# A decoder layer on one core: tokens instead of weights on the stationary side of the two MLP products

## The chip, the core and the metric

The kernel runs on one core of a Trainium2 chip. The metric is the device time in microseconds of one execution, as the median of three runs. The profile is of one further execution, taken by the hardware profiler; its span, from the first to the last instruction, is a little shorter than the device time of the same execution.

## What is computed

One layer of a hybrid decoder for 256 tokens (and 16 learned meta tokens ahead of them) of width 2048, all in float32. The part that matters here is the MLP at the end:

```
h = h + hybrid_mixer(rmsnorm(h, norm_mix_g), ...)        # two attention branches, gates, output projection
h = h + squared_relu_mlp(rmsnorm(h, norm_mlp_g), w1, w2)
return rmsnorm(h, final_norm_g)[:, 16:]

def squared_relu_mlp(xn, w1, w2):                         # w1: 2048 x 8192, w2: 8192 x 2048
    return square(relu(xn @ w1)) @ w2
```

The meta tokens are dropped, so the MLP works on 256 tokens.

## The kernel before

**Number format.** Every float32 operand is cut into an upper part `hi` (float32r) and a rest `lo`, and a product is the sum of hi·hi, hi·lo and lo·hi. ScalarE (ACT) makes `hi` with a cast, VectorE (DVE) makes `lo` with a subtraction.

**Layout.** Features lie on the partitions, tokens along the free dimension. A block of 128 output features and all 2048 input features is one weight *chunk* of 1 MB, stored as sixteen 128x128 tiles, one for each k-step `k`. The stationary operand of each matmul is a weight tile, the moving operand is the activation row `x[:, k]` with 512 columns: 256 tokens of `hi` and 256 of `lo`. `mac2` (L148) issues two matmuls for a k-step:

```
nc.tensor.matmul(steps(ps), hi, steps(row(x)), ...)                 # L149: weight hi, 512 columns
nc.tensor.matmul(steps(ps[:, 0:NT]), lo, steps(x[:, 0, :]), ...)    # L150: weight lo, 256 columns
```

`steps` (L141) reads and writes the columns in an order of four passes. `gemm2` (L160) does the 16 k-steps of a chunk into one PSUM bank. The left half of the bank and the right half are added afterwards.

**Weights.** `next_weights` (L131) takes the next chunk of one long list in two halves. Each half is one 512 KB transfer on the SyncE (SP) queue into a `raw` tile (L124; five of them), one cast on ACT (L126, 128x1024) and one subtraction on DVE (L127, 128x1024) into a `w` tile (five of them too).

**Stages.** The input products, the attention branches and the output projection come first (to about 845 us). The MLP then goes over four groups `g` of 2048 hidden features. In each group 16 chunks of `w1` give 16 hidden features blocks (operand `x2`), and 16 chunks of `w2` give 16 blocks of the output (operand `a`). A hidden block goes through `relu2` (L891): `total` adds the two halves of the bank (ACT copy L187, DVE add L190), DVE takes the maximum with zero times `r2b`, the row of inverse norms (L893), squares it (L895), and `split_to` writes hi (ACT, L194) and lo (DVE, L195) into `a`. An output block is added to the residual `h` by `add_residual` (L870: ACT copy L872, DVE adds L873 and L874).

**The end.** In the last group each of the output blocks 0 to 11 is also squared into `acc` (ACT L867, GpSimd (POOL) L868) and multiplied by the final gain (ACT L915). For the last four chunks the `lo` products come first (L927), with `hi` kept in `whi_last`, and then `half` (L931) does the `hi` products for 128 tokens after the other 128 (L943), so that the final norm of the first 128 tokens (`row`, L961: L967 sums `acc` over the partitions on TensorE) and their output go beside the products of the second.

**Order.** Each engine runs its own list in order. The lists are made by a scheduler that may move an instruction ahead of others on the same engine. Weight transfers are the only work of the SP queue in the MLP, and POOL's queue has none there.

## Time and profile before

| | |
|---|---|
| median of 3 runs | 1534.97 us (1534.77 to 1535.41) |
| the profiled execution | 1535.16 us |
| its span | 1533.5 us |
| TensorE clock granted | 0.998 |
| busy share of the span | PE 99%, weight load 91%, DVE 70%, ACT 52%, POOL 8% |
| read from HBM | 289.32 MB, 190 GB/s over the span |

How to read it: PE is TensorE's matmuls, PEld its weight loads (LDWEIGHTS), which overlap the matmuls. A matmul's duration in the profile is longer than the distance to the next one's start, because matmuls are pipelined; what a matmul costs is read from starts. In a group's row the numbers behind `|` are busy time, mean ns of one, and idle time of the engine just before the group's instructions with what ended it. The chain of waits is the sequence of work that ended last, followed back from the end.

### The profile page before, as it was taken

Reading aid. Unit: us, or ns where it says so; the run is one execution under the profiler, and the core shown is the slowest. Engines: PE = TensorE matmul, PEld = TensorE weight load, DVE = VectorE, ACT = ScalarE, POOL = GpSimd, SP = SyncE. Lnnn points to the kernel's source line nnn. Section 1 sums busy time; section 2 is a strip of 40 time slices with the busy share of each in tenths; the row PEclk is TensorE's granted clock in tenths of the full one; section 3 lists DMA queues with packets and bytes.
Section 4 is the critical chain, followed back from the end, with each engine's and each line's share of the span. In section 5 each row is a group of like instructions: output and inputs, shape, how many; then the busy total and the mean of one; then the engine's idle time right before and its main releaser. Section 6 shows DMA issues by size and latency. Waiting matters only on the chain.

```text
span 1533.5 us, 25353 instructions
## 1 busy us (share of the span) xinstructions
PE 1522.3 (99%) x9812; PEld 1399.9 (91%) x9812; DVE 1072.2 (70%) x1659; ACT 794.4 (52%) x1271; POOL 130.2 (8%) x213
## 2 busy tenths in 40 slices
PE   9999999999999999999999999999999999999997
PEld 8999999999999999999999999999999999999997
DVE  7898858586666666666787876667766776667665
ACT  7766444555555544544666544445444454444563
POOL 6012010111100000000011000000000000000012
PEclk9999999999999999999999999999999999999999
DMA  9545555565555565655565566655565556555562
GB/s 320 172 153 176 182 162 188 160 212 170 166 167 188 197 198 197 195 199 199 188 209 195 197 198 197 200 195 195 195 203 197 198 196 199 197 197 200 194 195 96
DMA packets 86600, 293.08 MB, mean 191 GB/s; under 512 B 9112, under 2 KB 16800, under 8 KB 86352
## 3 DMA queue, kind: packets, MB, share of 16 engines
q1 hardware_dynamic: 85872, 289.62, 57.4%
q8 instruction: 77, 1.26, 0.3%
q0 software_dynamic: 176, 1.12, 0.2%
q10 hardware_dynamic: 432, 0.72, 0.1%
q14 instruction: 43, 0.35, 0.1%
HBM read 289.32 MB, written 2.11 MB: 190 GB/s over the span
## 4 chain that ended last, share of the span: by engine, by line
PE 96%; DVE 2%; ACT 1%; issue 1%; DMA 0%; POOL 0%; SPq 0%; POOLq 0%; DVEq 0%; ACTq 0%
PE ps L149 50%; PE ps L150 26%; PE psa L154 5%; PE psa L158 4%; PE psa L156 4%; PE ps L364 1%; PE ps L943 1%; PE ps L366 1%; DVE w L127 1%; PE ps L927 0%; DMA raw<-w_all_dram 0%; PE pa L562 0%; PE po L620 0%; DVE room L434 0%; POOL o L991 0%
## 5 line engine op out<-in xcount | busy, mean ns | idle before, releaser
L127 DVE TENSOR_TENSOR w<-raw,w 128x1024 fp32r<-128x1024 f32 x522 | 644.8, 1235 | 260.5 <-ACT w L126 251.3
L126 ACT CAST w<-raw 128x1024 fp32r<-128x1024 f32 x522 | 547.1, 1048 | 275.2 <-PE ps L150 210.1
L149 PE MATMUL ps<-x,w 128*128 128x512 f32 x1952 | 654.7, 381 | 0.0
L150 PE MATMUL ps<-x,w 128*128 128x256 f32 x1952 | 535.7, 274 | 0.0
L149 PEld LDWEIGHTS ps<-x,w 128*128 128x128 f32 x1952 | 366.5, 188 | 62.4
L150 PEld LDWEIGHTS ps<-x,w 128*128 128x128 f32 x1952 | 366.7, 188 | 0.0
L149 PE MATMUL ps<-a,w 128*128 128x512 f32 x960 | 320.2, 380 | 0.0
L150 PE MATMUL ps<-a,w 128*128 128x256 f32 x960 | 263.3, 274 | 0.0
L149 PEld LDWEIGHTS ps<-a,w 128*128 128x128 f32 x960 | 180.3, 188 | 30.9
L154 PE MATMUL psa<-x,w 128*128 128x272 f32 x640 | 181.9, 285 | 0.0
L150 PEld LDWEIGHTS ps<-a,w 128*128 128x128 f32 x960 | 180.3, 188 | 0.0
L158 PE MATMUL psa<-x,w 128*128 128x272 f32 x640 | 179.8, 282 | 0.0
L156 PE MATMUL psa<-x,w 128*128 128x272 f32 x624 | 176.1, 282 | 0.0
L187 ACT COPY evb<-ps 128x256 f32<-128x256 f32 x160 | 59.4, 371 | 205.1 <-PE ps L150 203.5
L190 DVE TENSOR_TENSOR evt<-ps,evb 128x256 f32<-128x256 f32 x158 | 67.0, 424 | 80.1 <-ACT evb L187 79.7
L154 PEld LDWEIGHTS psa<-x,w 128*128 128x128 f32 x640 | 120.2, 188 | 0.2
L158 PEld LDWEIGHTS psa<-x,w 128*128 128x128 f32 x640 | 120.2, 188 | 0.1
L156 PEld LDWEIGHTS psa<-x,w 128*128 128x128 f32 x624 | 117.6, 188 | 0.0
L868 POOL TENSOR_TENSOR acc<-acc,hsq 128x256 f32<-128x256 f32 x26 | 26.5, 1017 | 737.6 <-ACT hsq L867 737.6
L149 PE MATMUL ps<-og,w 128*128 128x512 f32 x256 | 85.8, 380 | 0.0
L149 PE MATMUL ps<-y,w 128*128 128x512 f32 x256 | 85.4, 380 | 0.0
L872 ACT COPY evb<-ps 128x256 f32<-128x256 f32 x76 | 28.2, 371 | 103.3 <-PE ps L150 102.3
(297 smaller groups left out, 1471.2 us busy)
## 6 DMA issues: line engine op xcount, KB each, us to landing
raw<-w_all_dram SPq DMA_DIRECT2D x537, 512.0 KB, 4.5
raw<-w_all_dram SPq DMA_DIRECT2D x8, 384.0 KB, 6.7
h<-hT_dram SPq DMA_DIRECT2D x8, 275.0 KB, 6.8
negc<-fdram POOLq DMA_DIRECT2D x1, 1088.0 KB, 7.9
out_dram<-o SPq DMA_DIRECT2D x2, 512.0 KB, 2.6
raw<-w_all_dram SPq DMA_DIRECT2D x2, 256.0 KB, 3.7
room<-w_small_dram SPq DMA_DIRECT2D x1, 320.0 KB, 8.1
out_dram<-o ACTq DMA_DIRECT2D x1, 320.0 KB, 3.1
```

The source lines that it names most:

```text
L126: nc.scalar.copy(hi[:, k, :], r)
L127: nc.vector.tensor_tensor(lo[:, k, :], r, hi[:, k, :].bitcast(F32), op=ALU.subtract)
L149: nc.tensor.matmul(steps(ps), hi, steps(row(x)), start=first, stop=False)
L150: nc.tensor.matmul(steps(ps[:, 0:NT]), lo, steps(x[:, 0, :]), start=False, stop=last)
L154: nc.tensor.matmul(steps(ps[:, X_LO]), hi, steps(x_lo[:, k]), start=first, stop=False, skip_group_check=True)
L156: nc.tensor.matmul(steps(ps[:, 0:NA]), lo, steps(x_hi[:, k]), start=False, stop=last and hi is None, skip_group_check=True)
L158: nc.tensor.matmul(steps(ps[:, 0:NA]), hi, steps(x_hi[:, k]), start=False, stop=last, skip_group_check=True)
L187: nc.scalar.copy(b, ps[:, NT:512])
L190: nc.vector.tensor_tensor(t, ps[:, 0:NT], b, op=ALU.add)
L364: nc.tensor.matmul(steps(ps), hi, steps(row(x[:, k])), start=st, stop=False)
L868: nc.gpsimd.tensor_tensor(acc, acc, sq, op=ALU.add)
L872: nc.scalar.copy(b, ps[:, NT:512])
```

## The change

For both MLP products the sides are exchanged. The stationary operand is now a tile of 128 tokens and 128 input features (`x[:, k, o, P*t : P*t+P]`, token half `t`, `o` hi or lo), and the moving operand is a row of 512 weight columns, four chunks wide. `token_rows` does a *block* of four chunks: for each k-step and token half three matmuls of 512 columns, hi·hi, hi·lo and lo·hi, into one PSUM bank for each token half. With `n=2` two blocks go together: k-steps 0 to 11 of the one, 0 to 11 of the other, then 12 to 15 of each.

`wide_weights` loads, casts and subtracts two k-steps of four chunks at a time; a tile has the same 1024 columns a partition as before, in pieces of 256 columns (1 KB) from four chunks.

The products now have tokens on the partitions, so they are turned. `turn` transposes 32x32 squares on DVE into a tile, writes that to DRAM in four transfers and reads it back in one; all five are on POOL's queue. For the hidden features `hidden` does it per block, after ACT has taken relu with the scale `r2` (now one number per token and partition) and the square. For the output, `gathered` sums the rows of each block over the groups in `rows`, and turns each block once, at the last group for blocks 0 and 1 and at the last but one for blocks 2 and 3; POOL then adds them to `h`. The last group's output blocks 2 and 3 (chunks 8 to 15) are done as before, the last four of them in the two halves as before.

`norm2` sums over the partitions with the ones as moving operand (two columns). Start offsets of `x2`, `a`, `whi_last` and some weight tiles move by 32 columns. 32 chunks x 4 groups of matmuls become 30 blocks of token rows (16 for `w1`, 14 for `w2`) and 8 chunks of the old form.

```diff
+    def wide_weights(c0, q):
+        k0 = 4 * q
+        parts = []
+        for i in range(2):
+            raw = wp.tile([P, HK * P], F32, tag="raw", name=nm("raw"), bufs=RAW)
+            hi, lo = (t.rearrange("p k m -> p (k m)").rearrange("p (k c m) -> p k c m", k=2, m=P) for t in pair())
+            r = raw.rearrange("p (c k m) -> p c k m", k=2, m=P)
+            cols = slice((k0 + 2 * i) * P, (k0 + 2 * i + 2) * P)
+            nc.sync.dma_start(r, w_all[c0 : c0 + 4, :, cols].rearrange("c p (k m) -> p c k m", m=P))
+            r = r.rearrange("p c k m -> p k c m")
+            nc.scalar.copy(hi, r)
+            nc.vector.tensor_tensor(lo, r, hi.bitcast(F32), op=ALU.subtract)
+            parts.append([t.rearrange("p k c m -> p k (c m)") for t in (hi, lo)])
+        return lambda k: tuple(t[:, k % 2, :] for t in parts[k % 4 // 2])
...
-    x2 = operand(keep, "x2", at=56, tag="s2")
+    x2 = operand(keep, "x2", at=24, tag="s2")
...
+    def token_rows(x, n, between=None):
+        pts = [[bank(px, "pt") for _ in range(2)] for _ in range(n)]
+        for i, q in [(i, q) for i in range(n) for q in range(3)] + [(i, 3) for i in range(n)]:
+            w = wide_weights(chunk[0] + 4 * i, q)
+            for k in range(4 * q, 4 * q + 4):
+                hi, lo = w(k)
+                for t, ps in enumerate(pts[i]):
+                    xh, xl = (x[:, k, o, P * t : P * t + P] for o in range(2))
+                    nc.tensor.matmul(steps(ps), xh, steps(hi), start=(k == 0), stop=False)
+                    nc.tensor.matmul(steps(ps), xh, steps(lo), start=False, stop=False)
+                    nc.tensor.matmul(steps(ps), xl, steps(hi), start=False, stop=(k == KT - 1))
...
+    def turn(rows):
+        both = gat.tile([P, KT * P], F32, tag="o", name=nm("turn"))
+        for t, r in enumerate(rows):
+            nc.vector.transpose(both[:, 0:1024].rearrange("p (i t j r) -> p t i j r", i=4, t=2, r=32)[:, t],
+                                r().rearrange("p (j i s) -> p i j s", i=4, s=32))
+        back = both[:, 1024:]
+        there = dram.tile([P, 1024], F32, tag="there", name=nm("there"), bufs=2)
+        for c in range(4):
+            nc.gpsimd.dma_start(there.rearrange("(i s) (c e) -> c s i e", i=4, c=4)[c],
+                                both[32 * c : 32 * c + 32, 0:1024].rearrange("s (i e) -> s i e", i=4))
+        nc.gpsimd.dma_start(back, there)
+        return back.rearrange("p (c t j r) -> p j t c r", c=4, t=2, r=32)
+
+    def hidden(a, b, pt):
+        u = gat.tile([P, 2, 512], F32, tag="u", name=nm("u"), bufs=1)
+        def part(t):
+            nc.scalar.activation(u[:, t, :], pt[t], AF.Relu, scale=r2[:, 2 * t : 2 * t + 1])
+            nc.scalar.activation(u[:, t, :], u[:, t, :], AF.Square)
+            return u[:, t, :]
+        back = turn([lambda t=t: part(t) for t in range(2)])
+        for t in range(2):
+            hi, lo = (a[:, 4 * b : 4 * b + 4, o, P * t : P * t + P].rearrange("p j (c r) -> p j c r", r=32) for o in range(2))
+            split_to(hi, lo, back[:, :, t])
+
+    def gathered(g, b, pt):
+        rs = [rows[:, t, 512 * b : 512 * b + 512] for t in range(2)]
+        for r, ps in zip(rs, pt):
+            if g == 0:
+                nc.scalar.copy(r, ps)
+            else:
+                nc.vector.tensor_tensor(r, ps, r, op=ALU.add)
+        if g < (NG - 1 if b < 2 else NG - 2):
+            return
+        back = turn([lambda r=r: r for r in rs])
+        for j in range(4 * b, 4 * b + 4):
+            r = ht[:, j, :].rearrange("p (t c r) -> p t c r", t=2, r=32)
+            nc.gpsimd.tensor_tensor(r, r, back[:, j - 4 * b], op=ALU.add)
+            if b < 2:
+                normed(j)          # square_sum(j, acc) and the final gain
...
     for g in range(NG):
-        a = operand(keep, "a", at=16, tag="s1")
-        held = []
-        for f in range(KT):
-            ps = gemm2(next_weights(), x2, pool=px if g == 0 and f < 3 else pg)
...
-            relu2(a, f, ps)
-        last = g == NG - 1
-        for j in range(KT - NL if last else KT):
-            add_residual(j, gemm2(next_weights(), a))
...
+        a = operand(keep, "a", at=48, tag="s1")
+        for b in range(4):
+            hidden(a, b, *token_rows(x2, 1, norm2 if (g, b) == (0, 0) else None))
+        for b0, n in ((0, 2),) if g == NG - 1 else ((0, 2), (2, 1), (3, 1)):
+            for b, pt in enumerate(token_rows(a, n), b0):
+                gathered(g, b, pt)
+    for j in range(8, KT - NL):
+        add_residual(j, gemm2(next_weights(low=True), a))
+        normed(j)
```

**What TensorE has to do, in the middle of a group.** Before, the last k-step of one hidden block and the first of the next (`ps` is the PSUM bank; 128x4x32x4 is 512 columns, 128x4x16x4 is 256):

```order
L149 MATMUL ps_1427_9902<-x2_1211_8413,w_1426_9898 128x4x32x4
L150 MATMUL ps_1427_9902<-x2_1211_8413,w_1426_9898 128x4x16x4
L149 MATMUL ps_1435_9954<-x2_1211_8413,w_1432_9945 128x4x32x4
L150 MATMUL ps_1435_9954<-x2_1211_8413,w_1432_9945 128x4x16x4
L149 MATMUL ps_1435_9954<-x2_1211_8413,w_1432_9945 128x4x32x4
```

Now, one k-step of a block of four chunks and the start of the next (`pt` are the banks of the two token halves; L924, L925 and L926 are the three matmuls of `token_rows`):

```order
L924 MATMUL pt_1662_11798<-w_1671_11840,x2_1211_8413 128x4x32x4
L925 MATMUL pt_1662_11798<-w_1671_11840,x2_1211_8413 128x4x32x4
L926 MATMUL pt_1662_11798<-w_1671_11840,x2_1211_8413 128x4x32x4
L924 MATMUL pt_1663_11799<-w_1671_11840,x2_1211_8413 128x4x32x4
L925 MATMUL pt_1663_11799<-w_1671_11840,x2_1211_8413 128x4x32x4
L926 MATMUL pt_1663_11799<-w_1671_11840,x2_1211_8413 128x4x32x4
L924 MATMUL pt_1662_11798<-w_1673_11869,x2_1211_8413 128x4x32x4
```

Four chunks took eight matmuls for a k-step, half of them of 256 columns; they now take six, all of 512.

**What ACT has to do for the hidden features.** Before, for two hidden blocks of the last group (`evb` is the copy of the right half of the bank, `asq` the squared block):

```order
L126 CAST w_2037_14237<-raw_2036_14236 128x1024
L194 CAST a_2001_14022<-asq_2017_14123 128x256
L187 COPY evb_2023_14170<-ps_2022_14137 128x256
L126 CAST w_2043_14284<-raw_2042_14283 128x1024
L126 CAST w_2045_14289<-raw_2044_14288 128x1024
```

Now, from the end of the last block of the last group's hidden features (`u` is relu and its square, `turn` the tile that has been to DRAM and back, L952 the relu, L953 the square, L210 the cast into `a`):

```order
L952 ACTIVATE u_1883_13459<-pt_1865_13321,r2_9245 128x512
L952 ACTIVATE u_1883_13459<-pt_1866_13322,r2_9245 128x512
L152 CAST w_1899_13550<-raw_1898_13549 128x1024
L953 ACTIVATE u_1883_13459<-u_1883_13459 128x512 x2
L152 CAST w_1901_13555<-raw_1900_13554 128x1024
L152 CAST w_1903_13584<-raw_1902_13583 128x1024
L152 CAST w_1905_13589<-raw_1904_13588 128x1024
L152 CAST w_1907_13618<-raw_1906_13617 128x1024
L152 CAST w_1909_13623<-raw_1908_13622 128x1024
L210 CAST a_1801_12852<-turn_1884_13460 128x4x128 x2
L152 CAST w_1911_13652<-raw_1910_13651 128x1024
```

Between the square and the cast into `a` now stand five weight casts (L152); in that time the turn goes through DVE, POOL's queue and DRAM.

**What POOL has to do at the end.** Before, the squares of the last output blocks are added to `acc`:

```order
L868 TENSOR_TENSOR acc3_9246<-acc3_9246,hsq_2198_15360 128x256
L868 TENSOR_TENSOR acc3_9246<-acc3_9246,hsq_2205_15411 128x256
L868 TENSOR_TENSOR acc3_9246<-acc3_9246,hsq_2212_15462 128x256
L951 TENSOR_TENSOR acc3_9246<-acc3_9246,sq_2235_15601 128x128
L951 TENSOR_TENSOR acc3_9246<-acc3_9246,sq_2236_15623 128x128
```

Now the turns of output blocks 0 and 1 stand ahead of that (L942 to DRAM, L944 back, L976 the addition to `h`, L887 the addition of squares, eleven in all):

```order
L942 DMA there_1923_13758<-turn_1922_13755 32x4x256 x4
L942 DMA there_1928_13788<-turn_1927_13785 32x4x256 x4
L944 DMA turn_1922_13755<-there_1923_13758 128x1024
L944 DMA turn_1927_13785<-there_1928_13788 128x1024
L976 TENSOR_TENSOR h_80<-h_80,turn_1922_13755 128x256 x4
L976 TENSOR_TENSOR h_80<-h_80,turn_1927_13785 128x256 x4
L887 TENSOR_TENSOR acc3_9247<-acc3_9247,hsq_1924_13769 128x256
L887 TENSOR_TENSOR acc3_9247<-acc3_9247,hsq_1925_13774 128x256
L887 TENSOR_TENSOR acc3_9247<-acc3_9247,hsq_1926_13779 128x256
```

and on ACT the casts into `whi_last` for the last chunk now stand behind squares that wait for those additions, two `hsq` tiles being all there are (L886 the square, L982 the gain):

```order
L126 CAST whi_last_14018<-raw_1974_14081 128x1024
L886 ACTIVATE hsq_1926_13779<-h_80 128x256
L126 CAST whi_last_14018<-raw_1977_14104 128x1024
L886 ACTIVATE hsq_1929_13795<-h_80 128x256
L982 ACTIVATE h_80<-h_80 128x256
L886 ACTIVATE hsq_1930_13800<-h_80 128x256
L982 ACTIVATE h_80<-h_80 128x256
L126 CAST whi_last_14018<-raw_1979_14109 128x1024
```

Before, the additions of squares for the first eight output blocks were spread over the last group; now all eleven stand in its last four chunks.

More of the change, by code (lines that the diff above doesn't have):

```diff
@@ L882, in trunk @@
         square_sum(j, acc2)
-    r2b = keep.tile([P, NT], F32, tag="rb", name="r2b")
+    r2 = gat.tile([P, 4], F32, name="r2", bufs=1)
     def norm2():
-        root_of_sums(r2b, bank(px, "pn")[:, 0:NT], acc2, gat.tile([P, NT], F32, tag="n2", name="n2", bufs=1), 1.0 / D)
-    later(1, norm2)
-    def relu2(a, f, ps):
-        t = total(ps)
-        nc.vector.scalar_tensor_tensor(t, t, 0.0, r2b, op0=ALU.max, op1=ALU.mult)
-        s = gat.tile([P, NT], F32, tag="asq", name=nm("asq"))
-        nc.vector.tensor_tensor(s, t, t, op=ALU.mult)
-        split_to(a[:, f, 0, :], a[:, f, 1, :], s)
+        hi, lo = halves(NT)
+        split_to(hi, lo, acc2)
+        ps = bank(px, "pn")[:, 0:4]
+        for t in range(2):
+            for n, part in enumerate((hi, lo)):
+                nc.tensor.matmul(ps[:, 2 * t : 2 * t + 2], part[:, P * t : P * t + P], ones_r[:, 0:2],
+                                 start=(t == 0 and n == 0), stop=(n == 1), skip_group_check=True)
+        root(r2, ps, *(gat.tile([P, 4], F32, name=n, bufs=1) for n in ("r2v", "r2r")), 1.0 / D)
@@ new lines, in token_rows @@
+    def token_rows(x, n, between=None):
[9 more added lines that the diff above has]
+                    nc.tensor.matmul(steps(ps), xl, steps(hi), start=False, stop=(k == KT - 1))
+                if between and k == 6:
+                    between()
+        chunk[0] += 4 * n
+        issued()
+        return pts
```

36 lines of the change are left out of this document (17 added, 19 removed).

## The prediction

> **What bounds the kernel now.** I read the page's busy shares first, then the chain of waits, then TensorE's own waits, and then the matmuls' start times, since a matmul's recorded duration is no price.
>
> ```profile
> PE 1522.3 (99%) x9812; PEld 1399.9 (91%) x9812; DVE 1072.2 (70%) x1659; ACT 794.4 (52%) x1271; POOL 130.2 (8%) x213
> PE 96%; DVE 2%; ACT 1%; issue 1%; DMA 0%; POOL 0%; SPq 0%; POOLq 0%; DVEq 0%; ACTq 0%
> PE warm L328 <- DVE ones L214: 1.3, 1, 1.3
> PE ps L364 <- ACT w L297: 0.8, 3, 0.4
> PE pn L967 <- ACT sq L948: 0.7, 1, 0.7
> 1000.00:1100.00 100.00, 100.00 (x601) 90.34 (x601) 72.11 (x107) 49.80 (x73) 0.00 (x0) 1.00 0.59 197
> ```
>
> 96% of the chain is matmuls. The longest waits of TensorE in the whole program are about 1 us each, none of them in the MLP. In 100 us of the MLP it is busy for 100 us at clock 1.00, with DVE at 72%, ACT at 50% and the DMA engines at 59%. So the MLP takes what its matmuls take from start to start, and anything on another engine counts only once it makes TensorE wait.
>
> The starts, from the timeline of TensorE, in an output product of the last group:
>
> ```profile
> 1440.17 0.38 PE L149 MATMUL ps<-a,w 128*128 128x512 f32 x1
> 1440.39 0.27 PE L150 MATMUL ps<-a,w 128*128 128x256 f32 x1
> ...
> 1452.17 0.38 PE L149 MATMUL ps<-a,w 128*128 128x512 f32 x1
> ```
>
> 36 k-steps of a chunk take 12.00 us, 333.3 ns each. The 256-column matmul by itself stands in the chain near the end:
>
> ```profile
> 1510.59 7.26 PE ps L943 x64
> ```
>
> 7.26 us / 64 = 113.4 ns, so the 512-column one takes 333.3 - 113.4 = 219.9 ns. The difference of 106.5 ns for 256 columns is 0.416 ns a column; 113.4 - 106.5 leaves 6.9 ns that a matmul costs whatever its length.
>
> **The change part by part. The matmuls.** A k-step of four chunks was 4 x 333.3 = 1333.2 ns (3072 columns, eight matmuls). It is now 3072 columns in six matmuls of 512: 6 x 219.9 = 1319.4 ns, less by two fixed parts, 13.8 ns. There are 30 blocks of 16 k-steps, 480 in all: 480 x 13.8 ns = **-6.6 us**. A page of the Trainium skill (TensorE: Matmul & The Clock Gate, section "Back-to-back issue gap") gives the gap as N/2.4 + 2.5 ns, a fixed part of 2.5 ns; by it the sum would be 480 x 2 x 2.5 ns = -2.4 us. The rows above have 6.9 ns, and the measurement decides.
>
> All of this rests on 219.9 ns holding when a 512-column matmul follows another, which the MLP of before never does. The first stage does it in short runs (L364):
>
> ```profile
> 32.02 1.05 PE L364 MATMUL ps<-x,w 128*128 128x512 f32 x4
> 32.90 0.61 PE L366 MATMUL ps<-x,w 128*128 128x256 f32 x4
> ...
> 39.18 0.62 PE L364 MATMUL ps<-x,w 128*128 128x512 f32 x2
> 39.64 0.28 PE L154 MATMUL ps<-x,w 128*128 128x272 f32 x1
> ...
> 471.86 0.39 PE L149 MATMUL ps<-x,w 128*128 128x512 f32 x1
> 472.09 0.28 PE L150 MATMUL ps<-x,w 128*128 128x256 f32 x1
> 472.21 0.39 PE L149 MATMUL ps<-x,w 128*128 128x512 f32 x1
> ```
>
> A run of four takes 0.88 us, 220 ns each; a run of two after other shapes 0.46 us, 230 ns each; and at 472 us the alternating form itself holds 230 + 115 ns for a while before it falls back to 333. So there are two spacings, a short and a long one, and the short one is where long runs settle. I take 219.9 (bounds 213, the columns alone, and 230). Each ns more on a 512-column matmul costs 480 x 6 = 2880 ns, and at 222.2 ns the gain is gone.
>
> **The weights.** Each tile is still one transfer, one cast and one subtraction of 1024 columns, now in 1 KB pieces:
>
> ```profile
> L127 DVE TENSOR_TENSOR w<-raw,w 128x1024 fp32r<-128x1024 f32 x522 | 644.8, 1235 | 260.5 <-ACT w L126 251.3
> L126 ACT CAST w<-raw 128x1024 fp32r<-128x1024 f32 x522 | 547.1, 1048 | 275.2 <-PE ps L150 210.1
> 0.00:40.00 40.00, 37.95 (x217) 32.84 (x217) 28.93 (x42) 27.72 (x42) 24.02 (x49) 1.00 0.99 322
> raw<-w_all_dram SPq DMA_DIRECT2D x537, 512.0 KB, 4.5
> raw<-w_all_dram SPq DMA_DIRECT2D x8, 384.0 KB, 6.7
> ```
>
> The first 40 us load weights in just such pieces at 322 GB/s, against the 197 GB/s needed, plus about 50 GB/s for a turn's 1 MB per 21 us: some 0.77 of that rate. A tile lasts TensorE 2.64 us and there are five; less cast and subtraction a transfer has 5 x 2.64 - 2.3 = 10.9 us, and took 6.7 in the crowded stage. A block of 21.1 us has eight casts (8.4 us of ACT) and eight subtractions (9.9 us of DVE). Both read 128-column runs out of order, which no row shows; I take them at the same price. **Zero**, hidden under TensorE.
>
> **Turning a hidden block.** Nearest rows for pieces that were not there before:
>
> ```profile
> L632 ACT ACTIVATE so<-po 128x512 f32<-128x512 f32 x8 | 4.9, 616 | 0.0
> L195 DVE TENSOR_TENSOR v0l<-p,v0h 128x512 fp32r<-128x512 f32 x4 | 2.7, 685 | 0.0
> L464 POOL DMA_DIRECT2D fdram<-room x1 | 0.7, 705 | 5.0 <-DVE room L463 5.0
> fdram<-room POOLq DMA_DIRECT2D x1, 8.5 KB, 3.3
> ```
>
> Relu and square are 4 x 0.62 us with a cast of 1.05 between; the transposes I take as 2 x 0.69 (no row; half or double would not matter); four issues at 0.7, landing 3.3, the way back 0.7 + 4.5 (the 512 KB of a weight transfer): 2.5 + 1.05 + 1.4 + 2.8 + 3.3 + 0.7 + 4.5 = 16.2 us, and 2.6 for the four halves of the split. ACT comes to the split after five weight casts at TensorE's pace, 13.2 us, and may wait for some 3 us there, with the casts of the next tiles queued behind it, and DVE likewise. Those tiles are wanted only five tiles later, so TensorE doesn't feel it. The output product wants block 3 at its k-step 12, after 24 k-steps or 31.7 us, against 18.8. **Zero.** `relu2` and the additions of halves go away on ACT and DVE: no gain, they were hidden. `norm2` has four matmuls of two columns for two of 256: under 0.3 us.
>
> **The end.** With T the start of chunk 8 of the last group (1480.00 before):
>
> ```profile
> 1480.00 0.22 PE ps L149
> 1509.66 0.93 PE ps L927 x8
> 1517.85 0.44 PE pn L967 x4
> L868 POOL TENSOR_TENSOR acc<-acc,hsq 128x256 f32<-128x256 f32 x26 | 26.5, 1017 | 737.6 <-ACT hsq L867 737.6
> L880 DVE SCALAR_TENSOR_TENSOR x<-h,x x16: 485/964/968, 767.4 to 842.3; 128x256 fp32r<-128x256 f32 x16
> ```
>
> The last `lo` products are at T + 29.7 and the sum over `acc` at T + 37.9. Block 1 leaves TensorE at T: DVE adds and transposes by T + 2.8, POOL issues four transfers by T + 5.6 and the two ways back by T + 9.6 (landing at T + 8.9 ahead of the second), and both are home by T + 14.1. The eight additions of block 0 and 1 run from T + 10.8 to T + 19 at 1.02 us, the eleven of squares to T + 30, two of half the length to T + 31: 6.9 us before the sum needs them. ACT's last cast for `whi_last` waits for the third addition of squares, T + 22, so its `lo` is there at about T + 25.5, 4 us early. The last row warns: this DVE operation takes 485 ns alone and 964 while POOL adds. The Trainium skill (SBUF — State Buffer, section "Who interferes with whom") says that a DVE instruction with two SBUF inputs and a GpSimd instruction that reads SBUF exclude each other for their whole length; the row agrees. Nineteen additions in a row beside DVE's subtractions can so eat the margin: **+1 us** (0 to +8).
>
> Sum against the profiled execution: 1535.16 - 6.6 + 1.0 = 1529.6; it stood 0.2 us above the median, and its 1.7 us outside the span don't change. Against the median, **1529.4 us**.
>
> **The rivals.** 0.2% (3.1 us) is about what a measurement of this kernel can tell from no change.
>
> *The longer spacing holds.* In a stream of 512-column matmuls the moving operand is now a tile that ACT and DVE have just written, and every weight load falls into the first half of a matmul; if that keeps the 230 ns of 39.18, or some 225 between the two, the MLP gets longer: at 225, 2.8 x 2.88 = +8 us, 1543 us; at 230, +22.5 us, 1557 us. It decides from 222.2 ns on. For it speak the runs of two and the stretch at 472 us; against it the run of four, and that the long stretches all settled at 333.3.
>
> *The end waits for POOL.* If a POOL transfer took twice its two rows (issue 1.4 us, landing 6.6 us, way back 9 us), block 1's way back would land at about T + 27, the third addition of squares would end at T + 34, and the last `lo` at about T + 37.5 where TensorE wants it at T + 29.7: 8 us of waiting, 1536.4 us, no change. It decides from 4 us of lateness on. For it: two rows are thin, and DVE is busy; against: the 4 us.
>
> *The fixed part shrinks.* It may be a price of changing length, and go in an unbroken run of equal matmuls: 213.3 ns at the least would be 480 x (1333.2 - 1280) = -25.5 us, half of that 1522 us. The 2.5 ns of the Trainium skill's page (TensorE: Matmul & The Clock Gate, "Back-to-back issue gap") would mean 215.8 ns there, by which the time is 1517 us. The run of four at 220 speaks against it.
>
> *Cast or subtraction out of order.* If the subtraction took twice as long, DVE would have 8 x 2.47 = 19.8 us of them, 1.4 of transposes and 1.4 of splitting for a hidden block of 21.1 us and would set its pace: 16 x 1.5 = +24 us, 1559 us. The granted speed of runs of 128 in every row (time by element count alone) speaks against it.
>
> **How the numbers follow.** Forecast 0.53; longer spacing 0.22; the end waits 0.14; fixed part shrinks 0.06; DVE sets the pace 0.05. The range has to leave out two tenths: from 1526 (no wait at the end, and a ns to spare) to 1543 (225 ns); outside are the fixed part gone, over 225 ns, and DVE. Faster by over 0.2% (under 1531.9): forecast, fixed part and a little of the end, 0.60; within: most of the end and the longer spacing below 223.5 ns, 0.13; slower: 0.27.
>
> **What would show it.** Right: starts 220 ns apart in L924 to L926, 1.32 us from one k-step to the next, no TensorE wait over 0.5 us between 845 us and the last group's chunk 8, DVE and ACT less busy, DMA about 0.75 in the hidden products. Wrong: 222 ns and more between starts with no wait; a wait of L1006 or L1046 (the `lo` products and the sum of the end) for DVE or POOL; a wait for `w` (cast or subtraction) in the blocks.

## The result, and the profile after

The changed kernel takes 1548.53 us (median of 5 runs, 1547.05 to 1550.80) against 1534.97 us before (1534.77 to 1535.41): 1.0088 times as long, 95% interval 1.0073 to 1.0103, 13.6 us slower where 5.6 us faster was forecast. The profiled execution took 1548.53 us with a span of 1546.8, 13.3 us more than before. The lines below are the busy shares, the shares of the chain, the groups of weight casts and subtractions (L152 and L153 in the new form, beside the cast into `a`, L210), and the transfers of the turns.

```profile
PE 1527.4 (99%) x8854; PEld 1363.3 (88%) x8854; DVE 984.9 (64%) x1383; ACT 797.6 (52%) x1191; POOL 200.6 (13%) x329
PE 93%; DVE 2%; POOL 1%; issue 1%; DMA 1%; ACT 1%; SPq 0%; POOLq 0%; DVEq 0%; ACTq 0%
L153 DVE TENSOR_TENSOR w<-raw,w 128x1024 fp32r<-128x1024 f32 x240 | 293.2, 1225 | 260.1 <-ACT w L152 259.7
L152 ACT CAST w<-raw 128x1024 fp32r<-128x1024 f32 x240 | 250.1, 1045 | 269.5 <-PE pt L926 266.6 <-DVE w L153 1.6 <-PE ps L166 0.9
L210 ACT CAST a<-turn 128x512 fp32r<-128x512 f32 x32 | 18.3, 618 | 38.9 <-DMA turn<-there 38.9
there<-turn POOLq DMA_DIRECT2D x80, 128.0 KB, 4.7
turn<-there POOLq DMA_DIRECT2D x20, 512.0 KB, 5.3
```

DVE has 87 us less to do, as meant, and that is worth nothing, as forecast. The permuted cast and subtraction cost what the plain ones did (1.05 and 1.23 us). The transfers of a turn take 4.7 and 5.3 us instead of the 3.3 and 4.5 assumed. POOL and DMA have come into the chain with 1% each.

**Where the time went** is read from three marks of TensorE: the start of the first `lo` product of the end (L927 before, L1006 now), the start of the last sum over the partitions (L967, L1046), and the end of the span. First before, then after:

```profile
1501.17 2.02 PE L927 MATMUL ps<-a,w 128*128 128x256 f32 x16
1525.25 0.49 PE L967 MATMUL pn<-sq,ones 128*128 128x128 f32 x2 [0.67 <-ACT sq L948]
```

```profile
1503.98 0.75 PE L1006 MATMUL ps<-a,w 128*128 128x256 f32 x5
1533.10 0.49 PE L1046 MATMUL pn<-sq,ones 128*128 128x128 f32 x2 [0.67 <-ACT sq L1027]
```

Up to the first mark 2.8 us more, between the marks 5.0 us more (29.1 against 24.1), behind the last 5.5 us more (1546.8 - 1533.1 = 13.7 against 8.2). Each stretch has a cause of its own.

**The first stretch: the rhythm of the matmuls.** The timeline of TensorE around norm2's four matmuls of two columns (L911), and TensorE's row by window ahead of them and behind them (the number after x counts the matmuls that touch the window):

```profile
839.11 0.38 PE L924 MATMUL pt<-w,x 128*128 128x512 f32 x1
...
848.13 0.39 PE L926 MATMUL pt<-w,x 128*128 128x512 f32 x1
848.36 0.17 PE L911 MATMUL pn<-ones,csh 128*128 128x2 f32 x1
848.39 0.48 PE L924 MATMUL pt<-w,x 128*128 128x512 f32 x1
848.71 0.17 PE L911 MATMUL pn<-ones,csl 128*128 128x2 f32 x1
...
849.50 0.38 PE L924 MATMUL pt<-w,x 128*128 128x512 f32 x1
...
1482.43 0.38 PE L926 MATMUL pt<-w,a 128*128 128x512 f32 x1
1482.65 0.38 PE L165 MATMUL ps<-a,w 128*128 128x512 f32 x1
```

```profile
900.00:1000.00 100.00, 100.00 (x449) 1.00 0.71 220
1300.00:1400.00 100.00, 100.00 (x449) 1.00 0.72 227
```

42 matmuls from 839.11 to 848.13 are 9.02 / 41 = 220.0 ns apart. From 849.50 to 1482.43 there are 2835 more: 632.93 / 2834 = 223.3 ns. The distances alternate there, 222 and 225 ns, without a change at the boundaries of blocks, groups or operands. 2880 x 3.3 ns is 9.6 us; against the 6.6 us to be gained, that leaves a loss of 3 (the MLP also began 0.4 us earlier than before, hence 2.8 at the mark). Nothing waits: the forecast's 220 ns were there for 9 us, and were lost at 848 us.

**The second stretch: a wait, and the clock behind it.** TensorE's longest wait, ACT's and POOL's timeline around it, and TensorE by window with the granted clock behind its busy time:

```profile
PE ps L1006 <- DVE h L892: 3.3, 1, 3.3
1493.97 9.39 POOL L976 TENSOR_TENSOR h<-h,turn 128x256 f32<-128x256 f32 x8 [0.53 <-DMA turn<-there]
1503.31 8.25 POOL L887 TENSOR_TENSOR acc<-acc,hsq 128x256 f32<-128x256 f32 x7
1511.91 4.68 POOL L887 TENSOR_TENSOR acc<-acc,hsq 128x256 f32<-128x256 f32 x4 [0.35 <-ACT hsq L886]
1506.64 0.42 ACT L886 ACTIVATE hsq<-h 128x256 f32<-128x256 f32 x1 [0.35 <-POOL acc L887]
1507.37 1.03 ACT L126 CAST whi_last<-raw 128x1024 fp32r<-128x1024 f32 x1
1509.98 0.42 ACT L886 ACTIVATE hsq<-h 128x256 f32<-128x256 f32 x1 [0.87 <-POOL acc L887]
1510.31 0.35 ACT L891 COPY evb<-ps 128x256 f32<-128x256 f32 x1
1510.69 0.43 DVE L892 TENSOR_TENSOR h<-ps,h 128x256 f32<-128x256 f32 x1 [1.32 <-ACT evb L891]
1511.17 3.40 PE L1006 MATMUL ps<-a,w 128*128 128x256 f32 x16 [3.31 <-DVE h L892]
```

```profile
1508.00:1511.00 3.00, 0.00 (x0) 1.00 0.00 0
1511.00:1512.00 1.00, 0.83 (x5) 0.82 0.00 0
1512.00:1515.00 3.00, 3.00 (x16) 0.50 0.00 0
1515.00:1516.00 1.00, 1.00 (x10) 0.97 0.00 0
```

The third `lo` product needs the PSUM bank of output block 11 (three banks go round). That bank is free when ACT has copied its right half (`evb`) and DVE has added its left. ACT's copy stands behind squares, which wait for one of two `hsq` tiles, which POOL frees one addition at a time, after eight additions of turned blocks. So the next start came 3.6 us behind the last one (3.3 us of waiting by the view of waits), and then the clock stood at 0.50 for some 3.4 us: the 20 matmuls from 1511.17 to 1515.15 took 3.98 us instead of 20 x 0.114 = 2.3, another 1.7 us.

**The third stretch: POOL's closing DRAIN.** It isn't counted as busy; it stands in the view of the program's last line, here of before and of after (number, then shortest, middle and longest in ns):

```profile
L1069 POOLq DRAIN  x3: 40/93/1881, 1527.7 to 1533.2; - x3
```

```profile
L1148 POOLq DRAIN  x3: 40/245/10052, 1535.6 to 1546.6; - x3
```

It takes 8.2 us longer than before; the last output transfers cover a part, and the program's end moves by 5.5 us.

### The profile page after: what moved, and what is told of

It reads as the page before. It is cut to its first block, busy times and chain, and to the rows that moved or that the text cites. A ratio compares the mean times of both kernels' runs of the same rounds, so it can differ in the third digit from the quotient of the medians.

```text
span 1546.8 us, 23194 instructions
## 1 busy us (share of the span) xinstructions
PE 1527.4 (99%) x8854; PEld 1363.3 (88%) x8854; DVE 984.9 (64%) x1383; ACT 797.6 (52%) x1191; POOL 200.6 (13%) x329
## 4 chain that ended last, share of the span: by engine, by line
PE 93%; DVE 2%; POOL 1%; issue 1%; DMA 1%; ACT 1%; SPq 0%; POOLq 0%; DVEq 0%; ACTq 0%
PE ps L165 22%; PE pt L925 14%; PE pt L924 14%; PE pt L926 14%; PE ps L166 11%; PE psa L170 4%; PE psa L174 4%; PE psa L172 4%; PE ps L383 1%; PE ps L1022 1%; PE ps L385 1%; DVE w L127 1%; POOL h L976 1%; DMA turn<-there 0%; DMA raw<-w_all_dram 0%
## 5 line engine op out<-in xcount | busy, mean ns | idle before, releaser
L153 DVE TENSOR_TENSOR w<-raw,w 128x1024 fp32r<-128x1024 f32 x240 | 293.2, 1225 | 260.1 <-ACT w L152 259.7
L127 DVE TENSOR_TENSOR w<-raw,w 128x1024 fp32r<-128x1024 f32 x282 | 350.4, 1243 | 139.4 <-ACT w L126 137.2
L152 ACT CAST w<-raw 128x1024 fp32r<-128x1024 f32 x240 | 250.1, 1045 | 269.5 <-PE pt L926 266.6
L165 PE MATMUL ps<-x,w 128*128 128x512 f32 x928 | 313.0, 382 | 0.0
L166 PE MATMUL ps<-x,w 128*128 128x256 f32 x928 | 254.5, 274 | 0.0
L165 PEld LDWEIGHTS ps<-x,w 128*128 128x128 f32 x928 | 174.2, 188 | 29.6
L924 PE MATMUL pt<-w,x 128*128 128x512 f32 x512 | 196.4, 384 | 0.0
L925 PE MATMUL pt<-w,x 128*128 128x512 f32 x512 | 196.4, 384 | 0.0
L926 PE MATMUL pt<-w,x 128*128 128x512 f32 x512 | 196.3, 383 | 0.0
L166 PEld LDWEIGHTS ps<-x,w 128*128 128x128 f32 x928 | 174.2, 188 | 0.0
L924 PE MATMUL pt<-w,a 128*128 128x512 f32 x448 | 171.8, 384 | 0.0
L925 PE MATMUL pt<-w,a 128*128 128x512 f32 x448 | 171.8, 384 | 0.0
L926 PE MATMUL pt<-w,a 128*128 128x512 f32 x448 | 171.8, 384 | 0.0
L924 PEld LDWEIGHTS pt<-w,x 128*128 128x128 f32 x512 | 95.9, 187 | 18.4
L926 PEld LDWEIGHTS pt<-w,x 128*128 128x128 f32 x512 | 95.9, 187 | 18.4
```

The source lines that it names most:

```text
L127: nc.vector.tensor_tensor(lo[:, k, :], r, hi[:, k, :].bitcast(F32), op=ALU.subtract)
L152: nc.scalar.copy(hi, r)
L153: nc.vector.tensor_tensor(lo, r, hi.bitcast(F32), op=ALU.subtract)
L165: nc.tensor.matmul(steps(ps), hi, steps(row(x)), start=first, stop=False)
L924: nc.tensor.matmul(steps(ps), xh, steps(hi), start=(k == 0), stop=False)
L925: nc.tensor.matmul(steps(ps), xh, steps(lo), start=False, stop=False)
```

## The experiments

Theory: three separate costs, the rhythm (2.8 us here, against a gain of 6.6 forecast), the wait at the end with its clock (5.0), the DRAIN (5.5). The rivals stand in the expectations. The base is the changed kernel unless another is named. The last three columns of the table are the three stretches, read from the start times of one profiled execution of each kernel; all in us.

| kernel | median us | first `lo` product | to the last sum | to the end |
|---|---|---|---|---|
| before | 1534.97 | 1501.2 | 24.1 | 8.2 |
| changed | 1548.53 | 1504.0 | 29.1 | 13.7 |
| e2 turns on SP | 1543.76 | 1504.1 | 28.5 | 9.6 |
| e3 before, 64 transfers on POOL | 1537.05 | 1500.5 | 24.1 | 10.3 |
| e5 additions on DVE | 1544.79 | 1503.8 | 25.2 | 13.3 |
| e11 norm2 at k-step 11 | 1540.03 | 1494.8 | 29.8 | 13.7 |
| e12 all, ACT and POOL | 1534.74 | 1495.2 | 28.5 | 8.1 |
| e13 all, SP | 1533.34 | 1494.9 | 28.0 | 8.7 |
| e16 all, SP, later additions | 1531.03 | 1494.3 | 26.1 | 8.9 |

### The rhythm

**Offsets (s1, the survey).** One kernel, a different start of the weight tile in each block:

```diff
-    def wide_weights(c0, q):                    # hi at 24, lo at 24
+    def wide_weights(c0, q, at=(24, 24)):       # hidden block n: at=(4n, 4n); nine output blocks other pairs or orders
```

> Tokens on the stationary side as in the change, but each of the 16 hidden blocks starts its weight tiles (hi and lo parts alike) at another offset, 0, 4, 8 ... 60 numbers in place of 24, and nine of the output blocks use another pair of offsets, the columns in plain order instead of four passes (the first pair of blocks, and block 3 of the third group), or the three matmuls in the order hi-hi, lo-hi, hi-lo. Read is the mean distance of matmul starts in each block; the time as a whole is not compared. Theory 'offset': the 223.3 ns are a matter of where the moving tile starts against the stationary one, so blocks differ, some at 220 ns or below and some above 225. Rival 'form': 512 columns behind 512 columns cost 223.3 ns wherever the tiles lie, so all blocks are within 0.5 ns of 223.3, and only the order of columns or of matmuls could change it.

Mean distance in ns, by offset of hi and lo: 0: 226.9 (behind norm2's sums); 4: 230.0; 8: 226.5; 12: 228.1; **16: 220.0**; 20: 225.0; 24: 223.3; 28: 230.0; 32: 225.0; 36: 222.2; 40: 225.3; 44: 222.2; 48: 226.2; 52: 225.6; 56: 231.7; **60: 220.0**. hi 24 with lo 40: 220.0. Columns in plain order at 24: 228.9; the matmuls in the other order: 223.3. Blocks differ by up to 11.7 ns, so "form" was out and "offset" looked proven.

**Offset 16 (e4).**

```diff
-        a, b = (0, 20) if meta else (56, 56) if low else (24, 24)
+        a, b = (0, 20) if meta else (56, 56) if low else (at, at)     # at=16 in wide_weights
```

> The changed kernel with one number different: the weight tiles of the token rows (hi and lo) start at 16 instead of 24 numbers, 32 bytes earlier. Theory 'offset': 220.0 ns from start to start in all 30 blocks instead of 223.3, 2880 matmuls x 3.3 ns = 9.5 us less, the wait at the end and POOL's long DRAIN stay: 1539.0 us. Rival 'form': 223.3 ns as before, 1548.5 us.

1555.05 us, 1.0132 (1.0119 to 1.0146): neither value. All 30 blocks ran at 225.3 ns, at the addresses that had given 220.0 ns for a whole block in the run before:

```profile
900.00:1000.00 100.00, 100.00 (x445) 1.00 0.65 217
1300.00:1400.00 100.00, 100.00 (x446) 1.00 0.69 226
```

So addresses alone don't decide, and "offset" fell as well. What was left was the history: in the survey every block began with a change of offset.

**Knocks (e8).** Useless matmuls ahead of the third k-step of 21 blocks, all at offset 24:

```diff
+                if knock and k == 2:
+                    for _ in range(knock[0]):
+                        nc.tensor.matmul(dist[:, 0:knock[1]], x[:, k, 0, 0:P], hi[:, 0:knock[1]], start=True, stop=True)
```

> The changed kernel with extra matmuls of no use (into a PSUM bank that nobody reads) ahead of the third k-step of 15 hidden blocks and 6 output blocks: one to four of 2 columns, or one of 16, 32, 64 ... 512 columns. Read is the rhythm of starts behind each; the time as a whole is not compared. Theory 'rhythm': 512-column matmuls lock into one of several periodic patterns (220.0, 223.3, 225.3 ns in the mean), which one depends on how the stream was interrupted, and it stays until the next interruption; so the mean changes from block to block at the same addresses, and some blocks run at 220.0 ns. Rival 'addresses': start offsets alone decide, so every block comes back to 223.3 ns within a few matmuls.

Behind 5 of the 21 the stream ran at 220.0 ns to the next knock (one matmul of 16, 128 or 320 columns, and twice one of 256), behind 14 at 223.3 (a third one of 256 among them), behind 2 at 222.7. Nothing changed between knocks. So the rhythm is chosen at an interruption and stays, but the length of the knock alone doesn't choose it: four matmuls of 2 columns were followed by 223.3 ns twice and by 222.7 once.

**norm2 elsewhere (e9, and e11 timed).** In the change its sums are the only interruption of the stream:

```diff
-                if between and k == 6:
+                if between and k == 10:
```

> The changed kernel with the sums of norm2 (four matmuls of 2 columns) ahead of k-step 11 of the first hidden block instead of k-step 7. In the changed kernel the stream ran at 220.0 ns for the 42 matmuls up to them and at 223.3 ns for all 2837 behind them. Theory 'rhythm': 220.0 ns lasts for 66 matmuls here, up to the new place; what follows depends on where in the pattern they fall: 220.0 (time about 1539 us), 223.3 (1548.5 us) or another value. Rival 'a change at 848 us' (temperature, a transfer, another engine's work): 223.3 ns sets in at 848 us again, without an interruption there.

1539.88 us in a single execution. 220.0 ns up to the sums (now at 854 us) and 220.0 ns behind them, to the last block; the same two windows as above:

```profile
900.00:1000.00 100.00, 100.00 (x456) 1.00 0.67 220
1300.00:1400.00 100.00, 100.00 (x456) 1.00 0.73 235
```

The first `lo` product starts at 1494.9 us, 6.2 us ahead of the kernel before. The sums now stand together between two matmuls, where in the change the scheduler had put a 512-column one among them (848.39 above); which of the two, place or order, decides isn't told apart.

> The kernel with the sums of norm2 ahead of k-step 11 once more, timed. Theory 'rhythm, set by the order of the matmuls': every execution falls into the same rhythm, all times within 2 us of 1539.9. Rival 'drawn anew in each execution': times scattered over 1539.9, 1548.5 and 1555 us.

1540.03 us (1537.71 to 1542.35, 5 runs), 1.0033 (1.0020 to 1.0045), and 220.0 ns in the profiled execution again. The times spread by 4.6 us, a little more than the 2 us either way expected, but none lies near 1548: the rhythm is set by the program. All eight traces with the sums ahead of k-step 11 (e9, e11 to e17) show 220.0 ns behind them, and all four with the sums in their old place and nothing else done to the stream (the change, e1, e2, e5) show 223.3.

### POOL's closing DRAIN

The kernel before with 64 transfers on POOL that nobody needs, of 128 rows (e3) and then of 32 (e10):

```diff
         split_to(a[:, f, 0, :], a[:, f, 1, :], s)
+        nc.gpsimd.dma_start(away[f % 2], s)          # second kernel: s[0:32]
```

> The kernel before, with one transfer on POOL's queue for each hidden block (64 in all, the 128x256 tile asq to a DRAM tile that nobody reads). Theory: POOL's closing DRAIN grows with the number of transfers that POOL has issued, here 64 against 100 in the changed kernel: from 1.9 to about 7 us, time 1535 + 3.4 = about 1538.5 us (or 1540.4 if any number above a few gives the full 10 us). Rival 'POOL was behind with its additions': the drain stays under 2 us, 1535.0 us.

> The kernel before with 64 transfers on POOL's queue, as in the earlier run, but each of 32 rows of 1 KB instead of 128. There POOL's closing DRAIN took 7.11 us against 1.88 without them, 0.082 us for each transfer. Theory 'by transfers': 7.1 us again, about 1537 us. Rival 'by rows': a quarter of the increase, 3.2 us, which hides behind the last output transfers, 1535 us.

The first took 1537.05 us, 1.0014 (1.0005 to 1.0023), the second 1536.71 us in a single execution. DRAIN of the first and of the second:

```profile
L1072 POOLq DRAIN  x3: 40/102/7106, 1527.0 to 1534.6; - x3
```

```profile
L1071 POOLq DRAIN  x3: 40/102/7106, 1527.1 to 1534.7; - x3
```

The same 7.11 us: it goes by transfers and not by rows. The 20 transfers home of e12 (below) gave 3.51 us, the change's 100 gave 10.05. All three are 1.88 us + 0.082 us for each transfer. About the first 3 us of the growth hide behind the last output transfers (5.2 us longer cost 2.2 us).

The turns on SP's queue (e2):

```diff
-            nc.gpsimd.dma_start(there..., both[...])
-        nc.gpsimd.dma_start(back, there)
+            nc.sync.dma_start(there..., both[...])
+        nc.sync.dma_start(back, there)
```

> The five transfers of each turn go on SP's queue instead of POOL's; POOL's additions and everything else stay. Theory: POOL's closing DRAIN is long because of the transfers that POOL issued; without them it falls from 10.05 to about 2 us, 5.4 us less, and blocks 0 and 1 come home some us earlier, so that TensorE's wait at the end (3.3 us and the clock) shrinks or goes: 1538 to 1543 us. Rival 'POOL was behind': the drain stays at 10 us, 1546 to 1548 us. Rival 'weights queue behind the turns on SP': TensorE waits for w in the hidden blocks, over 1550 us.

1543.76 us, 1.0057 (1.0044 to 1.0069), just above the 1538 to 1543 expected. The DRAIN is back at 1.88 us with POOL's additions unchanged, so "POOL was behind" is out; the stretch behind the last sum is 4.1 us shorter and not 5.4, since 1.4 us more than before the change stay there (why is open). The wait at the end stays in another place (L1022 for L1007, 2.5 us).

### The wait at the end

**Nothing turned at the end (e1).** All output products of the last group in the old form:

```diff
-        if g < (NG - 1 if b < 2 else NG - 2):
+        if g < NG - 2:
-        for b0, n in ((0, 2),) if g == NG - 1 else ((0, 2), (2, 1), (3, 1)):
+        for b0, n in () if g == NG - 1 else ((0, 2), (2, 1), (3, 1)):
-    for j in range(8, KT - NL):
+    for j in range(KT - NL):
```

> The last group's output products are all made in the old form, and all four output blocks are turned in the last group but one: 28 blocks of token rows are left and POOL still has 20 turns in all. Theory (three parts: 3.0 us from the spacing of the stream, 5.0 to 5.4 from TensorE's wait for the eleventh block's addition at the end and the lower clock behind it, 5.4 from a longer DRAIN of POOL at the very end): the wait goes, the other two stay, 1534.97 + 3.0 + 5.4 = about 1543.4 us. Rival 'the drain is long because POOL was behind with its work at the end': the drain goes too, about 1538 us. Rival 'all of it is in the stream': 1548 us.

1551.64 us, 1.0113 (1.0099 to 1.0126): a miss for all three. The wait of L1006 went and the DRAIN stayed at 10.05 us, as the theory had it, but an output product in the old form wants the last hidden block in its k-step 13, after 4 us instead of 31.7:

```profile
PE ps L165 <- DVE a L211: 5.5, 1, 5.5
```

That is the price of a turn without cover; with 31.7 us of cover the prediction had it hidden, and in the change it was. The miss adds up: behind the wait the matmuls ran for another 4.5 us at a clock of 0.50, 2.3 us lost, and 1543.4 + 5.5 + 2.3 = 1551.2.

**DVE adds (e5).**

```diff
-            nc.gpsimd.tensor_tensor(r, r, back[:, j - 4 * b], op=ALU.add)
+            nc.vector.tensor_tensor(r, r, back[:, j - 4 * b], op=ALU.add)
```

> The changed kernel, but DVE instead of POOL adds the turned output blocks to h (16 additions, 8 of them at the end). Theory: TensorE's wait for the eleventh block's addition (3.5 us and 1.9 us at a lower clock) comes from ACT, whose copy of the right half stands behind squares that wait for POOL's chain of 8 + 11 additions; with 8 of them on DVE that chain is 9.4 us shorter and the wait goes: 1548.5 - 5.2 = about 1543.3 us, drain and spacing as before. Rival 'the transfers home are late whatever adds': DVE waits for the turned block with subtractions behind it, TensorE waits for w instead: 1546 to 1550 us.

1544.79 us, 1.0065 (1.0052 to 1.0078), 3.7 us less than the change, of the 5.2 us expected. L1006 no longer waits for L892. A wait of 0.9 us is left, and behind it the clock stays at 1.00:

```profile
PE ps L1022 <- DVE h L1007: 0.9, 1, 0.9
```

So in the change the chain over POOL's additions, ACT's squares and the copy was the cause.

### All three together

Two kernels combined offset 16 and DVE's additions with the turns on SP's (e6) or ACT's (e7) queue:

> Offset 16, additions on DVE, and the transfers of the turns on SP's queue. Theory: all three costs go and the shorter k-step is left: 1534.8 - 480 x 13.3 ns (6.4 us) + 0.3 + 1 (SP's queue at the end) = about 1529.5 us. Rival 'the end has another bound' (weight transfers behind the turns on SP, DVE's additions ahead of its subtractions): 1533 to 1537 us.

> As the run with SP's queue, but the transfers of the turns on ACT's queue. Theory: as there, about 1529 us, since ACT is busy for half of the time and its casts are five tiles ahead. Rival 'ACT waits for the transposes with the casts of the next tiles behind it': TensorE waits for w in the blocks, over 1535 us.

1546.48 us, 1.0082 (1.0068 to 1.0095), and 1549.98 us, 1.0098 (1.0083 to 1.0114). Both ran at 225.3 ns throughout: 2880 x 5.3 ns = 15.3 us of the misses of 17 and 21 us. The rest is waits at the end for DVE's additions out of the PSUM banks, 2.0 us in e6 and 4.8 in e7; TensorE waited for no `w`. With norm2 at k-step 11 instead, offset 24:

```diff
-                if between and k == 6:
+                if between and k == 10:
-            nc.gpsimd.tensor_tensor(r, r, back[:, j - 4 * b], op=ALU.add)
+            nc.vector.tensor_tensor(r, r, back[:, j - 4 * b], op=ALU.add)
-            nc.gpsimd.dma_start(there..., both[...])
+            nc.scalar.dma_start(there..., both[...])     # e13: nc.sync, for back too
```

> norm2 ahead of k-step 11, additions of the turned blocks on DVE, and of each turn the four transfers to DRAM on ACT's queue, the one back on POOL's (20 on POOL in all, a DRAIN of 1.9 + 20 x 0.082 = 3.5 us, hidden behind the last output transfers). Theory 'three costs, and they add': chunk 8 of the last group starts at 1473.5 us, 46.7 us from there to the last matmul as in the run with DVE's additions, 8.0 us and 1.7 us behind it as before the change: 1530.0 us, 4.8 us faster than before. Rival 'a fourth cost' (ACT waits for the transposes, the end has another bound): 1534 us or more.

> As the last, but all five transfers of a turn on SP's queue and none on POOL's. Theory 'three costs': 1530 us, or up to 1532.5 where the last weight transfers stand behind the two turns of the end. Rival 'a fourth cost': 1534 us or more.

e12: 1534.74 us, 1.0001 (0.9992 to 1.0010); e13: 1533.34 us, 0.9987 (0.9978 to 0.9996). The first and third stretch came out as forecast; in the second waits of 2.2 and 1.9 us, and 3.4 us of half clock behind each, were left (L1006 for L892, L1022 for L1007), with DVE busy for 4.5 to 5.0 of every 5 us there. By its time e12 lies where the rival had it (1534 us or more), and this is the rival's "the end has another bound". To take the end away altogether, the last group's output in the old form with its first three chunks interleaved (e14 with the turns on SP's queue, e15 split over ACT's and POOL's):

```diff
+    for j in range(3):                   # k-steps 0 to 11 of three chunks
+        held.append((bank(pg, "ps"), next_weights(low=True)))
+        for k in range(12):
+            mac2(held[j][0], *held[j][1](k), a[:, k], k == 0, False)
+    for j, (ps, w) in enumerate(held):   # then 12 to 15 of each
+        for k in range(12, KT):
+            mac2(ps, *w(k), a[:, k], False, k == KT - 1)
```

> The last group's output products wholly in the old form, so that nothing is turned at the end; its first three chunks do k-steps 0 to 11 one after the other and then 12 to 15 of each, 12 us in which the last hidden block comes home. norm2 ahead of k-step 11, turns on SP's queue, additions on POOL as in the changed kernel. Theory 'three costs': 448 k-steps of token rows at 1320 instead of 1333.3 ns are 6.0 us less, the end is that of the kernel before: 1534.9 - 6.0 = about 1529 us, up to 1530.5 with SP's queue at the end. Rival 'a fourth cost' that goes with the turns or with 512-column matmuls wherever they are: 1533 us or more. Rival 'twelve us are not enough': a wait of the 13th k-step for a, as in the run with the old end (5.5 us there), 1531 to 1535 us.

> As the last, but of each turn the four transfers to DRAM on ACT's queue and the one back on POOL's (20 on POOL). Theory 'three costs': about 1529 us, the DRAIN of 3.5 us hidden as in the earlier run with this split. Rivals as there: 1533 us or more.

1537.00 us, 1.0013 (1.0004 to 1.0022), and 1539.30 us, 1.0033 (1.0021 to 1.0046): the mechanism of the rival "twelve us are not enough", though above its 1531 to 1535 us, with waits of L165 for `a` of 5.1 and 9.9 us. Last, the change's products, but the additions, squares and gains of the turned blocks 0 and 1 written behind the last `lo` products:

```diff
         back = turn([lambda r=r: r for r in rs])
-        for j in range(4 * b, 4 * b + 4):        # add, square, gain
+        (at_end.append(home) if b < 2 else home())   # home() does that
...
         ends.append((j, w, ps))
+    for home in at_end:
+        home()
```

> norm2 ahead of k-step 11, turns on SP's queue, and the additions of the turned blocks 0 and 1 of the last group (on DVE), their squares and gains stand behind the additions of the last lo products in the program, so that ACT's squares and POOL's additions of them no longer stand ahead of casts, copies and subtractions of the last chunks. Theory 'three costs': with the wait at the end gone (1.9 us and some 1.7 us of the lower clock behind it in the run with SP's queue, 1533.3 us) the time is about 1529.7 us. Rival 'the sum over acc comes late': POOL's eight additions end behind the products of the first 128 tokens and the sum at the end waits, 1532 to 1535 us. Rival 'a fourth cost': no wait of TensorE over 0.7 us in the last 60 us and still 1533 us.

> As the last, with the transfers to DRAM on ACT's queue and those back on POOL's. Theory: about 1530 us (1534.7 in the run with this split, less 2.6 us of waits and 1.7 us of the lower clock). Rivals as there.

With SP's queue (e16) 1531.03 us, **0.9977 (0.9967 to 0.9986)**: faster than both kernels. The split over ACT and POOL (e17) gave 1535.76 us, 1.0005 (0.9996 to 1.0014), with 3.3 us of waits for L893 and 6.8 us of half clock left. TensorE's longest wait in the faster one:

```profile
PE ps L1016 <- DVE h L893: 1.4, 1, 1.4
```

Its first stretch is 6.8 us shorter than before the change, the second 2.0 longer (1.4 of it this wait), the third 0.7 longer: 4.1 us less in all, and 3.8 between the medians. No fourth cost is needed to explain the loss.

## Why the prediction was wrong

- **The matmuls, -6.6 us: this term failed first.** The price of a 512-column matmul was right (220.0 ns for 42 matmuls in the change, and for all 2880 with norm2 four k-steps later, where the first `lo` product is 6.2 us earlier than before). What failed is the step that let it hold for all 480 k-steps, and with it the line "norm2 has four matmuls of two columns for two of 256: under 0.3 us", which priced the sums by their own time alone. That time was right: 0.5 us (1.37 us from 848.13 to 849.50, less four times 0.22) against 0.2 for the two of 256. But they left the stream in a rhythm of 223.3 ns, 9.6 us.
- **"The short one is where long runs settle."** Wrong. There are more than two spacings (220.0, 222.2, 223.3, 225.3, 230.0 and others); 220.0, 223.3 and 225.3 ns each lasted for over 600 us, and the rows at 39 and 472 us, 230 ns for a while, were signs of it. The rival "longer spacing" had this, at 225 ns and 1543 us; it named the fresh tiles and the weight loads as the reason, and the runs show an interruption instead.
- **Weights, cast and subtraction out of order, turning a hidden block: zero.** Right. 1225 against 1243 ns; ACT waited 38.9 us in 16 turns, 2.4 us each, forecast 3; DMA at 0.73 to 0.77 in the four stretches of hidden products, forecast 0.75; no wait of TensorE in the blocks.
- **The end, +1 us (0 to +8): the mechanism named, the place and the size wrong.** POOL's first addition began 11.3 us behind the start of chunk 8 (forecast 10.8), the 11 squares ended 34 behind it (forecast 30). I asked when `whi_last` and the sum over `acc` are wanted (29.7 and 37.9). The copy `evb` of block 11, on the same queue behind the same squares, was wanted at 25, through a PSUM bank. And the wait took 1.7 us of clock along, which no row of before showed. 5.0 us instead of 1.0. The rival "the end waits for POOL" had 8 us and the waiting behind POOL's chain, but from transfers twice as long, which didn't come: the first addition came only 0.5 us later than forecast. That it named POOL is partly luck.
- **The DRAIN: missing altogether.** A queue was taken as free where nothing else was on it; each of POOL's 100 transfers was paid for once more in the closing DRAIN, 5.5 us of it behind the output.
- **The skill's rule.** The Trainium skill (TensorE: Matmul & The Clock Gate, "Back-to-back issue gap") gives N/2.4 + 2.5 ns as the gap of an isolated matmul, which for 512 columns is 215.8 ns. The shortest lasting rhythm here is 220.0 ns in the mean. The same page, "Part 1: The HAM clock gate", gives half clock after an idle window of about 3.4 us. Half clock came here behind shorter waits too, of 1.9 and 2.2 us (e13, e12), and not behind others of 2.0 to 2.9 us (last section).

## What to carry to other kernels

Where a kernel is bound by matmuls from start to start, measure the mean start distance over long stretches and on both sides of each interruption: a few small matmuls can choose the rhythm for the next 600 us. When work moves to the end of a kernel, list everything queued behind it on each engine and follow the PSUM banks, since the first thing wanted decides, not the last. Count the transfers on POOL's queue, too: each was paid for once more at the end here, 0.082 us.

## What the runs showed of the hardware

- 512-column float32r matmuls with a weight load each run in lasting periodic patterns with means from 220.0 to 231.7 ns. Start offsets and history together choose one: the change and e4 differ in the offset alone (24 and 16) and ran at 223.3 and 225.3 ns, the change and e9 in the place and order of four small matmuls alone and ran at 223.3 and 220.0. Offset 16 gave 220.0 ns in one block of the survey and 225.3 ns in three other kernels. Why isn't shown.
- POOL's closing DRAIN took 1.88 us + 0.082 us for each transfer that POOL had issued (20, 64 and 100 of them), whether of 32 rows or 128, and whether the last of them was issued 43 us before it (the change) or 86 us (e1, 10.05 us too).
- The length of a wait alone doesn't decide whether TensorE's clock falls. Behind 1.9 us in e13 it stood at 0.50 for 3.4 us; behind 2.0 us in e6 and 2.9 us in the survey it stayed at 1.00 (so it did behind 0.9 us in e5, 1.4 in e16, and 2.3 and 1.5 in e7). The longest waits of e13, e6 and the survey, each with the granted clock behind it:

```profile
PE ps L1022 <- DVE h L1007: 1.9, 1, 1.9
1501.30:1504.60 3.30, 3.30 (x18) 0.50 0.00 0
```

```profile
PE ps L1022 <- DVE h L1007: 2.0, 1, 2.0
1515.70:1522.00 6.30, 6.30 (x54) 1.00 0.01 3
```

```profile
PE ps L1019 <- DVE h L897: 2.9, 1, 2.9
1517.40:1524.00 6.60, 6.60 (x57) 1.00 0.01 2
```

In each trace of the change and its variants, the times at which the granted clock changes lie whole multiples of 3.41 us apart. Laid out in steps of that length from 1440 us to the last products, a clock of 1.00 fell to 0.50 behind every step in which TensorE stood idle for 1.87 us or more (1.94 in e13), and stayed at 1.00 behind those with up to 1.82 us (the survey's 2.9 us fell into two steps, 1.1 and 1.8). Where the steps lie against the program differs from trace to trace, so for a wait of 2 or 3 us the lost clock is partly luck.
